# Where the last raw block of the values lies, and when a block of output weights is opened, in a fused attention and gated-attention layer

## The chip, the cores and the metric

The kernel runs on one core of a Trainium2 chip. The metric is the device time of one execution in microseconds (us); lower is better. Three executions of the kernel before took 981.74, 981.85 and 983.63 us; the median, 981.85 us, is the number to compare with. A further execution was taken with the hardware profiler.

## The reference

One decoder layer over 1024 tokens of width 1024, in fp32. The input is normalized and multiplied by one wide matrix `w_in`; the columns of the product are the queries, keys, values and gates of eight differential softmax heads (`qa, ka, va, ga`) and of four gated linear heads (`qb, kb, vb, gb`, and a low-rank decay). Both results go through the output matrix and are added to the input:

```python
h = rms_norm(x, pre_g)
z = jnp.einsum('bsd,de->bse', h, w_in)
qa, ka, va, ga, qb, kb, vb, gb, gk_low = split_columns(z)
...
oa = diff_attention(qa, ka, va, lam)                 # softmax(q1 k1) - lam * softmax(q2 k2), times v
oa = rms_norm(oa, subln_g) * (1.0 - lam_init) * silu(ga)
log_a = log_sigmoid(gk_low @ w_gk_up + b_gk) / 16
ob = gla_chunked(qb, kb, vb, log_a)                  # S_t = diag(exp(log_a_t)) S_{t-1} + k_t^T v_t; o_t = q_t S_t
ob = rms_norm(ob, gla_g) * silu(gb)
y = jnp.einsum('bse,ed->bsd', jnp.concatenate([oa, ob], axis=-1), w_out)
return x + rms_norm(y, post_g)
```

## The kernel before

**Stages.** First the projections `h @ w_in` (until about 634 us of the span), with the gated heads computed in between; then scores, softmax and values of the eight attention heads together with the output product; then the last norm.

**Precision.** Every fp32 operand is split into a rounded part and a rest (`hi`, `lo`), and a product is three TensorE passes: hi with hi, hi with lo, lo with hi. A split takes a cast on ScalarE (ACT) and a subtraction on VectorE (DVE).

**Steps.** A projection is cut into 26 groups of columns (`pairs`, p = 0 to 25). Each is done by seven products instead of eight (a Strassen scheme) over the four quarters b11, b12, b21, b22 of its weights; `order` lists the steps (p, n), n = 1 to 7. A product n has its own left block of `h` and its own sum of weight quarters: n = 1 uses b11, n = 2 uses b21, n = 5 uses b12 - b11, n = 6 uses b22 - (b12 - b11), n = 7 uses b22 - b12, n = 4 uses b21 less the sum of n = 6, n = 3 uses b22. `go` (L682) runs the list: it makes the weights of up to three steps ahead (`prepare`), issues the matmuls of the step (`step`), lets `wo_step` do a piece of the output weights, and lets the generator `gla` of the gated heads do a piece.

**Values.** p = 22 and 23 (`VALS`) are the values of the attention heads. Both share one set of weights: eight raw loads of 512 KB, a half [0] and a half [1] of each of b11, b21, b12, b22 (`load_values`, L202, the DMA is L214, on SyncE's queue SP). `value_weights` (L291) makes the sums in place (L302, DVE), casts each half to hi (L306, ACT) and subtracts for lo (L309, DVE). hi and lo lie in a ring of five slots (`NRING`); a step's two hi and two lo take four of them, and a slot is free when the matmuls of both p = 22 and 23 that read it are done. `multiply_values` (L384) uses hi in its first two passes of eight matmuls and lo in the third.

**Places in memory.** The pool `kp` has the tags q0, q1, k0, k1, ks0, ks1 with one buffer each. They hold different tiles in turn; a new tile of a tag waits until every access to the one before it is done. During the gated heads q1 holds the decayed queries `gqd` (its other half serves `wo_step` as scratch, `spare`), ks0 the output `o` of the gated head ("go" in the profile), k1 a chain of small tiles that ends with the squares `sq_hl`, ks1 the gates ("gg"), q0 and k0 the keys, queries and values (`kq`, `gv`). The values' b12 goes to q0 and k0 and b22 to k1 and ks0. `o` is free when its last stores to `mixe` (L944) have landed; `gqd` is free when the last output matmul of the last gated head ("gpo") and the last use as scratch are done. At n = 7 the values keep two snapshots in `s3` (L483): in ks1 for p = 22, in q1 for p = 23. The same six tags then take the first attention head's queries and keys (`load_qk`, L954).

**Output weights.** `wo_step` (L663) splits `w_out` ahead of time in 32 blocks of 256 KB: one load into the single buffer `wo_raw` (L679, on GpSimd's queue POOL), a cast (L667, ACT), a subtraction (L669, DVE) and two stores to a DRAM copy (L671, POOL). A block is opened (loaded) at one step and closed (the rest) at a later one. Before the gated heads have begun, blocks are opened at n = 2 or 4 and closed at n = 1 or 6, and lo is written back into `wo_raw`, so that the next load waits for the store. Once `gqd` exists, lo goes to its free half, and each step with n = 1 or 6 closes one block and opens the next. The gated heads start right after the step (9, 3), that is at (10, 2).

**Order on the engines.** Matmuls are pinned in program order, and each block's load is pinned behind what precedes it on POOL. All other instructions are put in order by a planner that plays the program through on a timeline of its own, so an instruction stands in its engine's queue where the planner believed it would be ready. Each engine then runs its queue strictly in that order.

Of the kernel before, what the change touches and what calls it, by code (L numbers as in the profile page):

```python
# [8 lines left out]
F32 = mybir.dt.float32  # L9
# [5 lines left out]
P = 128  # L15
# [16 lines left out]
def hymba_kernel(  # L32
# [77 lines left out]
    def take_bank(shape, name):  # L110
        i = free.pop(0)
        return bank(i, shape, name), i
# [40 lines left out]
    kp = ctx.enter_context(tc.tile_pool(name="kp", bufs=1))  # L153
# [3 lines left out]
    def t2k(tag, bufs, name, dt=F32, shape=(P, 512)):  # L157
        return ap.tile(list(shape), dt, tag=tag, name=name, bufs=bufs)
# [17 lines left out]
    VALS = (len(pairs), len(pairs) + 1)  # L176
# [8 lines left out]
    def load_raw(p, halves=(0, 1)):  # L185
        if p >= len(pairs):
            return
        if p in VALS:
            return load_values("b11")
        c0 = pairs[p][2]  # L190
        for kh in halves:
            if kh not in raws.setdefault(p, {}):
                r = ap.tile([P, HB, 256], F32, tag="raw", name="w_raw", bufs=4)
                rows = slice(kh * 512, kh * 512 + 512)
                sp.dma_start(r, w_in[0, rows, c0 : c0 + 256].rearrange("(k p) c -> p k c", p=P))
                raws[p][kh] = r
# [5 lines left out]
    def load_values(name):  # L202

        if name not in value_raws:
            c0 = VA + (name[2] == "2") * 512
            r0 = (name[1] == "2") * 512
            value_raws[name] = []
            for i, tag in enumerate({"b12": ("q0", "k0"), "b22": ("k1", "ks0")}.get(name, ("raw",) * 2)):
                if tag == "raw":
                    r = ap.tile([P, 2, 512], F32, tag=tag, name="v_raw", bufs=4)  # L210
                else:
                    r = kp.tile([P, 2, 512], F32, tag=tag, name="v_raw")
                rows = slice(r0 + i * 256, r0 + i * 256 + 256)
                sp.dma_start(r, w_in[0, rows, c0 : c0 + 512].rearrange("(k p) c -> p k c", p=P))  # L214
                value_raws[name].append(r)

    EARLY = 5
    order = [(0, 1), (1, 1), (0, 2), (1, 2), (2, 1), (3, 1), (2, 2), (3, 2), (4, 1), (4, 2)]
# [16 lines left out]
    i = order.index((1, 4))  # L235
# [22 lines left out]
    def prepare(i):  # L258

        if i >= len(order) or i in ws:  # L260
            return
        if i < 4:

            act_ins, dve_ins = normed[0][:2]
            with tc.issue_after(act_ins.ins), tc.issue_after(dve_ins.ins):
                make_weights(i)
        else:
            make_weights(i)
# [115 lines left out]
    def multiply_values(i, pss, start):  # L384

        p, n = order[i]
        hi, lo = H[LEFT[n]]
        w = ws.pop(i)
        for j, (a, b) in enumerate(((0, hi), (0, lo), (1, hi))):
            for k in range(HB):  # L390
                for u, ps in enumerate(pss):
                    c = ((p - VALS[0]) * 2 + u) * P
                    mm(
                        ps, at(b, k)[:, c : c + P], w[a][k // 2][:, k % 2, :],
                        start=(start and j == 0 and k == 0), stop=(j == 2 and k == HB - 1),
                        skip_group_check=True,
                    )
# [60 lines left out]
    def take_heads(tile, unit, p0, p1):  # L458

        c, hi = t_c("c"), t_st("v_hi", F32R)  # L460
        lo = c.bitcast(F32R)
        dve.tensor_tensor(c, p0, p1, ALU.add)
        act.copy(hi, c)
        dve.tensor_tensor(lo, c, fp(hi), ALU.subtract)
        for t, src in enumerate((hi, lo)):
            sp.dma_start(
                v_d[unit][:, t, :, tile, :].rearrange("u p c -> p u c"),
                fp(src).rearrange("p (u c) -> p u c", c=P),
            )
# [3 lines left out]
    def step_values(i):  # L473

        p, n = order[i]
        state = sums.setdefault(p, [{}, {}])
        name = {1: "x", 2: "y", 5: "z", 6: "x", 4: "y", 7: "x", 3: "z"}[n]
        if n in (1, 2, 5, 4):
            for b in state:
                b[name], b["i" + name] = take_bank([P, 512], name)  # L480
        multiply_values(i, [b[name] for b in state], n not in (6, 7, 3))
        if n == 7:
            s3 = kp.tile([P, 2, 512], F32, tag="ks1" if p == VALS[0] else "q1", name="s3")  # L483
        for u, b in enumerate(state):
            t = (p - VALS[0]) * 2 + u
            ps = b[name]
            if n in (1, 6):
                k = "s1" if n == 1 else "s2"
                b[k] = t2k("s", 4, "s")
                act.copy(b[k], ps)  # L490
            elif n == 7:
                b["s3"] = s3[:, u]
                act.copy(b["s3"], ps)
                free.append(b["ix"])
                take_heads(4 + t, 1, b["z"], b["s3"])
            elif n != 5:
                half, unit, k = {2: (0, 0, "s1"), 4: (1, 0, "s3"), 3: (0, 1, "s2")}[n]
                take_heads(half * 4 + t, unit, ps, b[k])
                free.append(b["i" + name])

    def step(i):

        p, n = order[i]
        if p in VALS:
            return step_values(i)
        kind, m, _ = pairs[p]
        def snap(k, ps):
            other = k == "s3" and (wide(p) or p >= len(pairs) - 2)
            b[k] = t_c("s") if other else t2k("s", 4, "s")
            act.copy(b[k], ps)  # L510

        b = sums.setdefault(p, {})
        name = {1: "x", 2: "y", 5: "z", 6: "x", 4: "y", 7: "x", 3: "z"}[n]
        if n in (1, 2, 4, 5):
            b[name], b["i" + name] = take_bank([P, 512], name)
        ps = b[name]
        multiply(i, ps, n not in (6, 7, 3))

        def done(half, unit, p0, p1):
            if wide(p):  # L520
                return take_values(p, half, unit, p0, p1)
            c = t_c("c")
            dve.tensor_tensor(c, p0, p1, ALU.add)
            take(kind, m, half, unit, c)

        if n == 1:
            snap("s1", ps)
        elif n == 2:
            done(0, 0, ps, b["s1"])
            free.append(b["iy"])  # L530
        elif n == 6:
            snap("s2", ps)
        elif n == 7:
            snap("s3", ps)
            free.append(b["ix"])
            done(1, 1, b["z"], b["s3"])
            done(1, 0, b["y"], b["s3"])
            free.append(b["iy"])
        elif n == 3:
            done(0, 1, ps, b["s2"])  # L540
            free.append(b["iz"])
# [121 lines left out]
    def wo_step(n):  # L663
        if n in (1, 6) and wo_open:
            e, dh, raw = wo_open.pop()
            hi = t_c("wo_hi", F32R)
            act.copy(hi, raw)  # L667
            lo = (spare[0][:, 1] if spare else raw).bitcast(F32R)
            dve.tensor_tensor(lo, raw, fp(hi), ALU.subtract)  # L669
            for t, src in enumerate((hi, lo)):  # L670
                pool.dma_start(wod[e][t][:, cols(dh)], fp(src))  # L671
        if n in ((1, 6) if spare else (2, 4)) and wo_todo and not wo_open:
            e, dh = wo_todo.pop(0)
            raw = ap.tile([P, 512], F32, tag="t4", name="wo_raw", bufs=1)
            src = w_out[0, e * P : (e + 1) * P, cols(dh)]
            if len(wo_todo) == 31:
                sp.dma_start(raw, src)
            else:
                tc.keep_in_program_order(pool.dma_start(raw, src))  # L679
            wo_open.append((e, dh, raw))  # L680

    def go(n):  # L682
        for _ in range(n):
            i = made[0]
            if i == len(order):
                return
            made[0] = i + 1
            for a in range(4):
                prepare(i + a)
            step(i)  # L690
            if order[i][0] >= EARLY and order[i][0] not in VALS:
                wo_step(order[i][1])
            for _ in range(2 if order[i][0] in VALS else 1):
                if fill and next(fill[0], 0) == 0:
                    fill.pop(0)
# [3 lines left out]
    for i in range(1, 4):  # L699
        prepare(i)  # L700
    go(1)
    first(1)
    go(2)
    norm_x(4, 5)
    norm_x(6, 7)
    go(1)
    for j in range(HB):
        blocks(j)
# [905 lines left out]
```

## Time and profile before

| | |
|---|---|
| median of three executions | 981.85 us |
| the profiled execution | 983.51 us, of which its span (first to last instruction) 981.8 us |
| TensorE (PE) busy | 954.9 us, 97% |
| VectorE (DVE), ScalarE (ACT), GpSimd (POOL) busy | 734.3, 602.6, 187.7 us |
| mean granted TensorE clock | 0.997 |
| DMA | 220.39 MB, mean 224 GB/s |

How to read the rows further down. A row of a timeline has the start and the length in us, the engine, the line, the operation, its output and inputs, and how many were merged ("x8"); in brackets stands how long the engine had been idle before it and what ended that. "SPq" and "POOLq" are the queues that issue DMAs; the length there is the issue, not the transfer. A row of waits has who waited for whom, the us in total, how often, and the longest. A row of windows has the window, its length, the busy time of each engine, then the granted TensorE clock (1.00 is full speed), the share of the DMA engines and GB/s. A row of the chain of waits has start, length and what the last-ending work was at that time.

### The profile page before, as it was taken

The numbers are of one execution on the slowest core, as the hardware profiler recorded it, in microseconds if no ns is written. First come the engines' busy times: TensorE is split into PE (matmuls) and PEld (weight loads), VectorE is DVE, ScalarE is ACT, GpSimd is POOL, SyncE is SP. The second block draws the span as 40 slices with busy tenths as digits, with TensorE's granted clock in tenths as the row PEclk, the third lists the DMA queues.
The fourth block names the chain that finished last, engine by engine and source line by source line (L and its number), as shares of the span: only waits on it lengthen the run. The fifth ranks groups of instructions, "written<-read, shape, count | busy, mean of one in ns | idle before, by whom it ended". The sixth has DMA issues, their size and how long they took to land.

```text
span 981.8 us, 14991 instructions
## 1 busy us (share of the span) xinstructions
PE 954.9 (97%) x4946; PEld 812.4 (83%) x4946; DVE 734.3 (75%) x1452; ACT 602.6 (61%) x1164; POOL 187.7 (19%) x253
## 2 busy tenths in 40 slices
PE   6999999998999999999999899999999999999997
PEld 5998988887888888888888688878888888888785
DVE  6887598896677787677666567487888888898554
ACT  8642454754667456567665244366777687787773
POOL 5200001111111111122100002121322322343321
PEclk9999999999999999999999999999999999999999
DMA  9442456477676979886663489997746659995777
GB/s 353 141 117 89 133 171 221 172 234 279 216 234 217 306 240 305 274 281 224 235 193 108 140 249 282 396 281 239 234 153 231 230 200 359 341 282 115 150 204 150
DMA packets 152141, 220.39 MB, mean 224 GB/s; under 512 B 16592, under 2 KB 87248, under 8 KB 151968
## 3 DMA queue, kind: packets, MB, share of 16 engines
q1 hardware_dynamic: 138128, 178.80, 56.7%
q0 software_dynamic: 13936, 40.64, 13.9%
q8 instruction: 39, 0.64, 0.3%
q14 instruction: 38, 0.31, 0.1%
HBM read 133.93 MB, written 88.60 MB: 227 GB/s over the span
## 4 chain that ended last, share of the span: by engine, by line
PE 83%; DMA 6%; issue 4%; DVE 4%; ACT 1%; POOL 1%; SPq 0%; DVEq 0%; POOLq 0%; ACTq 0%
PE x L117 20%; PE ypart L117 13%; PE y L117 12%; PE z L117 11%; PE sc L117 7%; PE po L117 5%; PE yps L117 4%; PE wtr L120 3%; PE gpo L117 3%; DMA wo_d<-wo_raw 3%; DMA wo_raw<-in_w_out_dram 2%; PE kv L117 1%; DMA w_raw<-in_w_in_dram 1%; PE gkl_ps L117 1%; PE pa L117 1%
## 5 line engine op out<-in xcount | busy, mean ns | idle before, releaser
L352 ACT CAST w<-w_raw 128x512 fp32r<-128x512 f32 (+1 forms) x150 | 98.0, 655 | 99.1 <-PE y L117 42.3
L353 DVE TENSOR_TENSOR w<-w_raw,w 128x512 fp32r<-128x512 f32 (+1 forms) x150 | 109.6, 732 | 40.2 <-ACT w L352 39.6
L1137 ACT ACTIVATE p<-p,stt 128x896 f32<-128x896 f32 (+7 forms) x128 | 99.3, 777 | 36.8 <-DVE stt L1127 35.7
L510 ACT COPY s<-x 128x512 f32<-128x512 f32 x72 | 42.2, 586 | 71.3 <-PE x L117 71.0
L1127 DVE CUSTOM_DVE_ANT_0 p<-sc,maskt 128x512 f32<-128x512 f32 (+3 forms) x128 | 74.2, 585 | 14.3 <-PE sc L117 12.8
L1143 POOL TENSOR_SCALAR p<-p,stt,lam 128x1024 f32<-128x1024 f32 (+3 forms) x64 | 56.5, 882 | 146.5 <-DVE stt L1142 144.7
L117 PE MATMUL x<-s_hi,w 128*128 128x512 f32 x320 | 80.2, 393 | 2.5 <-ACT s L510 2.5
L117 PE MATMUL z<-s_hi,w 128*128 128x512 f32 x320 | 80.1, 392 | 0.0
L117 PE MATMUL y<-h_hi,w 128*128 128x512 f32 x320 | 80.0, 392 | 0.0
L117 PE MATMUL ypart<-wo_hi,m_hi 128*128 128x512 f32 x192 | 79.5, 414 | 0.1
L671 POOL DMA_DIRECT2D wo_d<-wo_hi x32 | 17.6, 551 | 318.6 <-ACT wo_hi L667 318.6
L117 PE MATMUL ypart<-wo_hi,m_lo 128*128 128x512 f32 x192 | 75.5, 393 | 0.0
L117 PE MATMUL ypart<-wo_lo,m_hi 128*128 128x512 f32 x192 | 75.4, 393 | 0.0
L333 DVE TENSOR_TENSOR w_raw<-w_raw 128x512 f32<-128x512 f32 (+1 forms) x88 | 65.6, 746 | 10.6 <-DMA w_raw<-in_w_in_dram 9.4
L117 PEld LDWEIGHTS x<-s_hi,w 128*128 128x128 f32 x320 | 59.6, 188 | 15.1 <-ACT s L510 2.9
L117 PE MATMUL sc<-k,q 128*128 128x512 f32 (+1 forms) x192 | 69.0, 363 | 1.3 <-DVE stt L1127 1.3
L117 PEld LDWEIGHTS y<-h_hi,w 128*128 128x128 f32 x320 | 59.7, 188 | 12.2
L117 PEld LDWEIGHTS z<-s_hi,w 128*128 128x128 f32 x320 | 59.6, 188 | 12.2
L117 PE MATMUL sc<-ks,q 128*128 128x512 f32 (+1 forms) x192 | 66.1, 347 | 0.0
L1185 ACT CAST wt_hi<-wtr 128x512 fp32r<-128x512 f32 (+1 forms) x80 | 42.8, 535 | 25.5 <-PE wtr L120 24.8
L1186 DVE TENSOR_TENSOR wt_lo<-wtr,wt_hi 128x512 fp32r<-128x512 f32 (+1 forms) x80 | 50.6, 632 | 9.0 <-ACT wt_hi L1185 8.5
L1146 DVE SCALAR_TENSOR_TENSOR p<-p,stt,p 128x1024 f32<-128x1024 f32 (+3 forms) x64 | 52.1, 814 | 5.1 <-POOL p L1143 4.8
(236 smaller groups left out, 2307.7 us busy)
## 6 DMA issues: line engine op xcount, KB each, us to landing
w_raw<-in_w_in_dram SPq DMA_DIRECT2D x48, 512.0 KB, 4.7
wo_d<-wo_hi POOLq DMA_DIRECT2D x32, 256.0 KB, 2.9
q<-q_d SPq DMA_DIRECT2D x32, 256.0 KB, 4.8
k<-k_d SPq DMA_DIRECT2D x32, 256.0 KB, 5.7
ks<-k_d SPq DMA_DIRECT2D x64, 128.0 KB, 5.7
v<-v_d SPq DMA_DIRECT2D x16, 512.0 KB, 6.8
wo_raw<-in_w_out_dram POOLq DMA_DIRECT2D x31, 256.0 KB, 4.3
wo_d<-gqd POOLq DMA_DIRECT2D x22, 256.0 KB, 3.8
```

The costliest lines, as they stand in the source:

```text
L117: tc.keep_in_program_order(pe.matmul(*a, **k))
L120: tc.keep_in_program_order(pe.transpose(dst, src, ident))
L333: dve.tensor_tensor(dst, a, b, ALU.subtract)
L352: act.copy(w[0], src)
L353: dve.tensor_tensor(w[1], src, fp(w[0]), ALU.subtract)
L510: act.copy(b[k], ps)
L1127: ins = dve.tensor_tensor_reduce(p[:, a:e], sc[:, : e - a], maskt[:, NZ + P - (e - a) :] if last else maskt[:, : e - a], 1.0, 3e38 if i == ...
L1137: act.activation(p[:, :n], p[:, :n], AF.Exp, bias=st[:, m : m + 1], scale=-1.0, accum_out=st[:, 2 + m : 3 + m],)
L1143: pool.tensor_scalar(p1[:, :n], p1[:, :n], st[:, 5:6], lam, ALU.mult, ALU.mult)
L1146: dve.scalar_tensor_tensor(p0[:, :n], p0[:, :n], st[:, 4:5], p1[:, :n], ALU.mult, ALU.subtract)
L1185: act.copy(hi[:, :n], pt[:, :n])
L1186: dve.tensor_tensor(lo[:, :n], pt[:, :n], fp(hi[:, :n]), ALU.subtract)
```

## The change

Three lines. The second half of the values' b22 goes to the buffer q1 instead of ks0. The snapshot `s3` of p = 23, which was in q1, goes to ks0. And `wo_step` is left out at the step (9, 4), where it opened a block four steps ahead of the gated heads.

```diff
-            for i, tag in enumerate({"b12": ("q0", "k0"), "b22": ("k1", "ks0")}.get(name, ("raw",) * 2)):
+            for i, tag in enumerate({"b12": ("q0", "k0"), "b22": ("k1", "q1")}.get(name, ("raw",) * 2)):
...
-            s3 = kp.tile([P, 2, 512], F32, tag="ks1" if p == VALS[0] else "q1", name="s3")
+            s3 = kp.tile([P, 2, 512], F32, tag="ks1" if p == VALS[0] else "ks0", name="s3")
...
-            if order[i][0] >= EARLY and order[i][0] not in VALS:
+            if order[i][0] >= EARLY and order[i][0] not in VALS and order[i] != (9, 4):
                 wo_step(order[i][1])
```

In terms of blocks: with the blocks counted from 0, block 9 was opened at (9, 4) and closed at (10, 1), and block 10 was opened at (10, 2). Now block 9 is opened at (10, 2), and every later block moves up by one place in the list of steps. Block 31, which was opened at (20, 6) and closed at (21, 1), is opened at (21, 1) and closed at (21, 6). The number of blocks, loads and stores stays the same.

## The prediction

> **What bounds the kernel now.** I read the page's first line and its chain first, then what PE waits for, then the neighbourhood of each long wait.
>
> ```profile
> PE 954.9 (97%) x4946; PEld 812.4 (83%) x4946; DVE 734.3 (75%) x1452; ACT 602.6 (61%) x1164; POOL 187.7 (19%) x253
> PE 83%; DMA 6%; issue 4%; DVE 4%; ACT 1%; POOL 1%; SPq 0%; DVEq 0%; POOLq 0%; ACTq 0%
> ```
>
> PE is the bound: an edit pays only where PE stands still. The waits of PE, longest first:
>
> ```profile
> PE xT L120 <- DVE x L565: 8.7, 4, 7.3
> PE x L117 <- ACT w L306: 3.8, 1, 3.8
> PE x L117 <- ACT s L510: 2.5, 1, 2.5
> ```
>
> The first is the start of the kernel. The two others lie where this change works: ACT w L306 casts a weight of the values, ACT s L510 copies a sum next to the output weights. PE around the first of them:
>
> ```profile
> 543.60 1.98 PE L117 MATMUL z<-w,s_lo 128*128 128x512 f32 x8
> ...
> 547.23 1.07 PE L117 MATMUL x<-w,s_hi 128*128 128x512 f32 x4
> 552.10 1.65 PE L117 MATMUL x<-w,s_hi 128*128 128x512 f32 x4 [3.80 <-ACT w L306]
> ...
> 556.55 3.81 PE L117 MATMUL x<-w,s_hi 128*128 128x512 f32 x16
> ```
>
> From 543.60 to 547.23 run sixteen matmuls (eight of them in the row left out): 3.63 / 16 = 0.227 us each. The values' product n = 6 begins at 547.23, runs four matmuls on the first half of its weights, to 547.23 + 0.91 = 548.14, and stands until the second half is cast. The next starts at 552.10: **3.96 us idle**. Then twelve matmuls take 556.55 - 552.10 = 4.45 us where 2.72 would do: **1.73 us more**. The windows say why:
>
> ```profile
> 548.00:552.00 4.00, 0.30 (x2) 0.00 (x0) 2.31 (x3) 1.00 (x2) 0.00 (x0) 1.00 0.16 61
> 552.00:556.00 4.00, 3.90 (x10) 3.11 (x11) 3.46 (x4) 1.00 (x2) 0.00 (x0) 0.58 0.11 20
> ```
>
> The granted clock after the gap is 0.58; 4.00 x 0.42 = 1.68 us of pulses are missing, which fits. Together the place costs 3.96 + 1.73 = 5.69 us. What it waits for, in the chain of waits:
>
> ```profile
> 543.08 2.25 DMA mixe<-go
> ...
> 545.40 4.27 DMA v_raw<-in_w_in_dram
> ...
> 551.00 1.05 ACT w L306
> ```
>
> The last store of the gated heads' output must land before ks0 may be overwritten; only then, at 545.40, goes the load of b22[1]; DVE makes the sum, ACT casts it, PE goes on.
>
> **The change, part by part.**
>
> *b22[1] into q1.* The last reader of q1, and the loads of b12[1] and b22[0]:
>
> ```profile
> 516.40 0.39 PE L117 MATMUL gpo<-gqd,gu 128*128 128x128 f32 x2
> ...
> 516.60 0.38 SPq L214 DMA_DIRECT2D v_raw<-in_w_in_dram  x1
> ...
> 531.01 0.38 SPq L214 DMA_DIRECT2D v_raw<-in_w_in_dram  x1
> ```
>
> q1 is read for the last time at 516.40 + 0.39 = 516.8; k0 comes free with the same matmuls, and b12[1] leaves for it at 516.60. The scratch half of q1 is done with earlier (below). So b22[1] can leave right behind b12[1], or, if the planner keeps the order of the code, right behind b22[0] at 531.4. Its flight is bounded by the eight loads of this kind:
>
> ```profile
> DMA to landing us min/median/max: 3.6/3.9/5.5
> ```
>
> It lands by 531.4 + 5.5 = 536.9. What is late next? DVE:
>
> ```profile
> 538.30 1.22 DVE L309 TENSOR_TENSOR w<-v_raw,w 128x1024 fp32r<-128x1024 f32 x1
> ...
> 541.23 1.22 DVE L302 TENSOR_TENSOR v_raw<-v_raw 128x1024 f32<-128x1024 f32 x1
> ...
> 544.17 1.22 DVE L302 TENSOR_TENSOR v_raw<-v_raw 128x1024 f32<-128x1024 f32 x1
> 549.69 3.50 DVE L302 TENSOR_TENSOR v_raw<-v_raw 128x1024 f32<-128x1024 f32 x3 [4.30 <-DMA v_raw<-in_w_in_dram]
> 553.10 2.35 DVE L309 TENSOR_TENSOR w<-v_raw,w 128x1024 fp32r<-128x1024 f32 x2
> ```
>
> By the order of the code I read 538.30 as the last use of the old sum in b11[1], 541.23 as the first half of the new one, and the first of the three at 549.69 as the half that PE lacks. The bracket at 549.69 says that DVE stood 4.30 us for the load, so it was at work until 545.39. If the planner now puts the missing sum right behind 541.23, it ends at about 543.7; if it puts it at the end of that run, at 545.39 + 1.22 = 546.6. The cast (1.05) needs a ring slot as well: the first to come free is that of n = 5's first half, four matmuls into the pass at 543.60, at 544.5. So the second half is ready between 544.5 + 1.05 = 545.6 and 546.6 + 1.05 = 547.7, and PE wants it at 548.14. The lo halves follow: behind 546.6 one more sum (1.22), then two subtractions, the first done at 549.0, the second at 550.2. PE's third pass starts at 547.23 + 16 x 0.227 = 550.9 and wants the second half 0.9 later. **PE does not stop, and the 5.69 us go whole**; the tightest margin is 0.4 us. If DVE does one more sum first (the third of 549.69 may come early now), PE stands 1.22 - 0.4 = 0.8 us.
>
> Would a shorter rest of the gap also pay for the clock? The other gap, before 226.38, did not:
>
> ```profile
> 226.00:230.00 4.00, 3.62 (x16) 3.02 (x17) 3.24 (x5) 1.94 (x5) 1.09 (x3) 1.00 0.53 210
> ```
>
> So 2.50 us of waiting left the clock at 1.00 and 3.96 us of idling did not; by the rows a rest of 3 us would cost between 3.0 and 4.7. The Trainium skill, "TensorE: Matmul & The Clock Gate", section "What's actually happening", lets the clock fall after about 3.4 us of idling; by that a rest of 3 us would cost 3.0, the lower end. Both gaps here agree with it.
>
> *s3 into ks0.* The snapshot of p = 23 is written here:
>
> ```profile
> 574.67 0.59 ACT L493 COPY s<-x 128x512 f32<-128x512 f32 x1 [1.39 <-PE x L117]
> ```
>
> ks0's stores have landed by 545.4, so it waits for nothing. Afterwards q1 and ks0 have changed roles under the first attention head's loads, which may move one of them by a microsecond or two. The cover is long, from the last issue (593.32 + 1.97 = 595.3) to the first use:
>
> ```profile
> 593.32 1.97 SPq L966 DMA_DIRECT2D ks<-k_d  x3
> ...
> 636.29 0.40 PE L117 MATMUL sc<-k,q 128*128 128x512 f32 x1
> ```
>
> *No block at (9, 4).* The blocks run late on their one buffer:
>
> ```profile
> L671 POOL DMA_DIRECT2D wo_d<-wo_raw x10: 539/539/567, 143.5 to 234.9; - x10
> ...
> 229.98 0.55 POOL L679 DMA_DIRECT2D wo_raw<-in_w_out_dram  x1 [2.59 <-DMA wo_d<-wo_raw]
> ...
> 239.95 0.55 POOL L679 DMA_DIRECT2D wo_raw<-in_w_out_dram  x1 [4.53 <-DMA wo_d<-wo_raw]
> ```
>
> Ten stores leave `wo_raw`, those of blocks 0 to 9, the last at 234.9; so 229.98 is block 9's load and 239.95 block 10's. Block 9 with its load, cast, subtraction and two stores now belongs to (10, 2) and (10, 6), and block 10 no longer waits 4.53 us for a store. ACT's casts of blocks 8 and 10:
>
> ```profile
> 225.22 0.62 ACT L667 CAST wo_hi<-wo_raw 128x512 fp32r<-128x512 f32 x1 [6.12 <-DMA wo_raw<-in_w_out_dram]
> ...
> 244.50 0.62 ACT L667 CAST wo_hi<-wo_raw 128x512 fp32r<-128x512 f32 x1 [2.22 <-DMA wo_raw<-in_w_out_dram]
> ```
>
> PE's 2.50 us before 226.38 come from the first: it stands in ACT's queue ahead of the copy that PE needs. But that is block 8, opened at (9, 2), ahead of the edit, and the planner works forward in time; I take the stall as unchanged, **0**, with -2.5 us if those two change places and +2.5 if such an order arises anew. The wait at 244.50 should shrink; PE did not wait there, and gains nothing.
>
> At the far end block 31 comes four steps later, about where these stand:
>
> ```profile
> 489.01 0.54 POOL L671 DMA_DIRECT2D wo_d<-gqd  x1 [0.95 <-DVE gqd L669]
> ...
> 506.49 0.62 ACT L352 CAST w<-w_raw 128x512 fp32r<-128x512 f32 x1 [4.85 <-PE x L117]
> wo_raw<-in_w_out_dram POOLq DMA_DIRECT2D x31, 256.0 KB, 4.3
> ```
>
> Its load can leave behind 489.01 and is there by about 494. ACT has 4.85 us free before 506.49 for one cast. Stores that leave by 507.5, with the load's 4.3 us for their flight, are down by 512, before the 516.8 at which q1 comes free anyway. Without that cover b22[1] would still have until 531.
>
> *Sum.* -5.69 + 0 + 0. The profiled execution took 983.51 us with a span of 981.8: 983.51 - 5.69 = 977.8, span 976.1. The median of the runs is 1.66 us lower: 981.85 - 5.69 = **976.2 us**. Behind 552 no wait of PE is longer than those quoted at the top, and the later loads hang on PE's own progress, so the gain is kept.
>
> **Rivals.**
>
> *Part is lost to crowding.* b22[1] beside b12[1] delays the latter, and DVE's and ACT's queues stand behind it:
>
> ```profile
> 520.17 1.23 DVE L302 TENSOR_TENSOR v_raw<-v_raw 128x1024 f32<-128x1024 f32 x1 [7.19 <-DMA v_raw<-in_w_in_dram]
> ...
> 523.69 1.03 ACT L306 CAST w<-v_raw 128x1024 fp32r<-128x1024 f32 x1
> ...
> 524.80 1.98 PE L117 MATMUL y<-w,h_hi 128*128 128x512 f32 x8
> ```
>
> Behind 520.17 comes the sum of the gated head's squares, behind its cast on ACT the cast at 523.69, done at 524.7; PE wants that half four matmuls after 524.80, at 525.7. If both loads shared evenly, b12[1] would land 3.6 us later and PE stand 3.6 - 1.0 = 2.6 us: 978.8, or 980.5 if the clock falls too. Against: SP issues b12[1] first. With the 0.8 us of DVE above, this case is 977 to 980.5; chance 0.15. The Trainium skill, "DMA: Bandwidth & Descriptors", section "Bandwidth", measures 6.15 us for 1 MB; by that, as an estimate, the slip would be 2.5 us and PE's loss 1.5. No pair of such loads stands alone in this trace.
>
> *The stall at 226 goes too*, by a new order on ACT: 976.2 - 2.5 = 973.7; chance 0.07.
>
> *The change doesn't do what it says.* The load may use q1 but keep its place in SP's queue, behind these stores:
>
> ```profile
> 543.68 1.13 SPq L466 DMA_DIRECT2D v_d<-c  x2
> ```
>
> It would leave at 544.8, 0.6 us earlier than now: 981.2. For: the queue's order is the planner's. Against: b12[1] left within 0.2 us of its buffer's release. Chance 0.08.
>
> *Slower.* The planner deals the casts L667 of blocks 9 to 31 anew, and they stand in front of a copy L510 while their block has not landed, as block 8's does. Place: ACT's queue from 226 to 506; price 2.5 us each; it outweighs the gain from the third on (3 x 2.5 = 7.5). Four would give 976.2 + 10 = 986.2. Against: from (10, 6) on the steps that open and close are the same as before, and of the two late loads quoted only one stopped PE. Chance 0.10.
>
> **How the numbers follow.** Forecast, chance 0.60: 976.2, by itself 975.2 to 977.2 (DVE's 0.8 us and as much the other way). The range, 973.4 to 980.6, reaches from the stall at 226 to crowding with the clock, and leaves out the case of no effect and the slower one (0.18). A measurement of this kernel can tell about 0.2% (2 us) from no change. Faster by more than that: the forecast, the stall at 226 and most of crowding, 0.81. Within it: no effect and the rest of crowding, 0.09. Slower: 0.10.
>
> **What would show it.** Right: a load L214 leaves between 516 and 532 and none behind the `mixe` stores; no wait of PE on ACT w L306; the clock is 1.00 from 540 to 560; nine stores out of `wo_raw`. Wrong: a wait of PE between 517 and 530 (crowding), on L510 at a new place (dealing), or near 548 for DVE's sums.

## The result and the profile after

Six executions of the changed kernel took 974.86 to 978.85 us, **median 977.18 us**; six of the kernel before took 981.74 to 983.63 us, median 982.57. The ratio is **0.9944, 95% interval 0.9928 to 0.996**: 5.4 us less, with 3.9 to 7.1 us inside the interval. The forecast was 976.2 us within 973.4 to 980.6, and faster. The profiled execution of the changed kernel took 977.31 us, with a span of 975.6 us and a mean granted clock of 0.997; before these were 983.51, 981.8 and 0.997.

The page's first line and its chain, after (PEld is TensorE's loading of weights):

```profile
PE 953.7 (98%) x4946; PEld 811.4 (83%) x4946; DVE 734.2 (75%) x1452; ACT 602.7 (62%) x1164; POOL 188.1 (19%) x253
...
PE 84%; DMA 5%; issue 4%; DVE 4%; ACT 1%; POOL 1%; SPq 0%; DVEq 0%; POOLq 0%; ACTq 0%
```

The same number of instructions on every engine, nearly the same busy times: no work was removed, PE only stands less. Its waits, after:

```profile
PE xT L120 <- DVE x L565: 8.8, 4, 7.1
PE x L117 <- ACT s L510: 1.9, 1, 1.9
PE y L117 <- DVE s L648: 1.3, 1, 1.3
```

The wait on the values' cast (w L306), the second longest before, is no longer there. The one on the copy (s L510) is. The timeline of PE at the values' n = 6, after:

```profile
545.46 1.98 PE L117 MATMUL z<-w,s_hi 128*128 128x512 f32 x8
547.28 1.98 PE L117 MATMUL x<-w,s_hi 128*128 128x512 f32 x8
549.09 1.98 PE L117 MATMUL x<-w,s_lo 128*128 128x512 f32 x8
```

n = 6 begins at 547.28 (547.23 before) and now runs eight matmuls through where it ran four and stood. The windows of after, one ahead of it and two on the stretch that was lost before (the busy times are those of PE, PEld, DVE, ACT and POOL, in this order):

```profile
544.00:548.00 4.00, 4.00 (x20) 3.30 (x19) 4.00 (x6) 1.58 (x2) 0.00 (x0) 1.00 0.69 205
548.00:552.00 4.00, 4.00 (x19) 3.34 (x18) 2.00 (x2) 0.53 (x1) 0.00 (x0) 1.00 0.51 147
552.00:556.00 4.00, 4.00 (x19) 3.30 (x19) 0.00 (x0) 1.44 (x3) 0.00 (x0) 1.00 0.38 119
```

PE is busy for 4.00 of 4.00 us at clock 1.00; before, the second window held 0.30 us of work and the third ran at 0.58. The cause is in SP's queue, after:

```profile
516.67 0.90 SPq L214 DMA_DIRECT2D v_raw<-in_w_in_dram  x2
...
531.09 0.37 SPq L214 DMA_DIRECT2D v_raw<-in_w_in_dram  x1
...
543.14 0.36 SPq L944 DMA_DIRECT2D mixe<-go  x1
```

At 516.67 leave two raw loads where before there was one: b12[1] and right behind it b22[1]. Behind the last `mixe` store no load L214 follows.

**Where the 6.2 us of the spans come from.** Setting the start of every matmul beside that of the same matmul before gives the running difference: -0.94 us from the first 20 us on (the start of the kernel, which differs from execution to execution), **+1.01 us at the stall near 226**, **-5.72 us at the values' n = 6**, -0.5 us when the attention heads begin, near 657. The sum is -6.2. The second term shows a flaw in my reading; here is its place after, first PE, then its windows:

```profile
221.87 1.07 PE L117 MATMUL y<-h_lo,w 128*128 128x512 f32 x4
224.82 2.62 PE L117 MATMUL x<-s_hi,w 128*128 128x512 f32 x8 [1.89 <-ACT s L510]
```

```profile
222.00:226.00 4.00, 2.12 (x10) 1.42 (x9) 1.37 (x3) 2.15 (x4) 1.08 (x2) 1.00 0.99 353
226.00:230.00 4.00, 4.00 (x13) 3.13 (x12) 2.19 (x5) 0.81 (x2) 0.55 (x1) 0.57 0.40 149
```

PE waited less than before (1.89 us, not 2.50), but this time the granted clock behind it fell to 0.57: 4.00 x 0.43 = 1.7 us of pulses are missing.

### The profile page after: what moved, and what is told of

The parts are those of the page before. It is cut to its first block, busy times and chain, and to the rows that moved or that the text cites. A ratio compares the mean times of both kernels' runs of the same rounds, so it can differ in the third digit from the quotient of the medians.

```text
span 975.6 us, 14993 instructions
## 1 busy us (share of the span) xinstructions
PE 953.7 (98%) x4946; PEld 811.4 (83%) x4946; DVE 734.2 (75%) x1452; ACT 602.7 (62%) x1164; POOL 188.1 (19%) x253
## 4 chain that ended last, share of the span: by engine, by line
PE 84%; DMA 5%; issue 4%; DVE 4%; ACT 1%; POOL 1%; SPq 0%; DVEq 0%; POOLq 0%; ACTq 0%
PE x L117 20%; PE ypart L117 13%; PE y L117 12%; PE z L117 12%; PE sc L117 7%; PE po L117 5%; PE yps L117 4%; PE wtr L120 3%; PE gpo L117 3%; DMA wo_d<-wo_raw 2%; PE kv L117 1%; DMA wo_raw<-in_w_out_dram 1%; PE gkl_ps L117 1%; PE pa L117 1%; DMA k_d<-qk_st 1%
## 5 line engine op out<-in xcount | busy, mean ns | idle before, releaser
L510 ACT COPY s<-x 128x512 f32<-128x512 f32 x72 | 42.2, 586 | 73.9 <-PE x L117 73.4
L117 PE MATMUL x<-s_hi,w 128*128 128x512 f32 x320 | 80.7, 394 | 1.9 <-ACT s L510 1.9
L117 PE MATMUL z<-s_hi,w 128*128 128x512 f32 x320 | 80.1, 392 | 0.0
L117 PE MATMUL y<-h_hi,w 128*128 128x512 f32 x320 | 80.0, 392 | 0.0
L117 PE MATMUL ypart<-wo_hi,m_hi 128*128 128x512 f32 x192 | 79.6, 414 | 0.1
L117 PE MATMUL ypart<-wo_hi,m_lo 128*128 128x512 f32 x192 | 75.5, 393 | 0.0
L117 PE MATMUL ypart<-wo_lo,m_hi 128*128 128x512 f32 x192 | 75.4, 393 | 0.0
L117 PEld LDWEIGHTS x<-s_hi,w 128*128 128x128 f32 x320 | 59.8, 188 | 14.6 <-ACT s L510 2.3
L117 PE MATMUL sc<-k,q 128*128 128x512 f32 (+1 forms) x192 | 69.0, 363 | 1.2 <-DVE stt L1127 1.2
L117 PEld LDWEIGHTS y<-h_hi,w 128*128 128x128 f32 x320 | 59.7, 188 | 12.2
L117 PEld LDWEIGHTS z<-s_hi,w 128*128 128x128 f32 x320 | 59.6, 188 | 12.2
L117 PE MATMUL sc<-ks,q 128*128 128x512 f32 (+1 forms) x192 | 66.1, 347 | 0.1
```

What stands on the lines that cost most here:

```text
L117: tc.keep_in_program_order(pe.matmul(*a, **k))
```

## The experiments

The theory T: the gain is the values' stop alone, made by the first two lines of the change (the buffers); the third line is worth nothing by itself, and the stall near 226 is a separate matter that the change leaves alone. The rivals: the third line has a part in the gain, by fewer waits for the stores (R1); or what matters is only that the load comes earlier at all, so that a load that still leaves behind the stores would do nearly as well in another buffer (R2). Each ratio is to the kernel before on the same chip in the same series. No kernel leaves work out.

### The parts alone

`e1_b22_only` keeps the two lines on the buffers and takes the third back; `e2_wo_only` is the reverse.

```diff
 e1_b22_only, against the changed kernel
-            if order[i][0] >= EARLY and order[i][0] not in VALS and order[i] != (9, 4):
+            if order[i][0] >= EARLY and order[i][0] not in VALS:
 e2_wo_only, against the changed kernel
-            ... {"b12": ("q0", "k0"), "b22": ("k1", "q1")} ...
+            ... {"b12": ("q0", "k0"), "b22": ("k1", "ks0")} ...
-            s3 = kp.tile([P, 2, 512], F32, tag="ks1" if p == VALS[0] else "ks0", name="s3")
+            s3 = kp.tile([P, 2, 512], F32, tag="ks1" if p == VALS[0] else "q1", name="s3")
```

> Only the two buffer lines of the change; the block of output weights is still opened at (9, 4). If the whole gain is the load of b22[1] that no longer waits for the gated heads' stores, this kernel gains as much as the full change, 5.7 us against the kernel before (5 to 6.5): PE has no wait on ACT w L306 near 548, the clock is 1.00 from 540 to 560, and the load leaves right behind b12[1] near 517. If the block of output weights carries part of the gain, this one falls short by that part (over 1 us).

> Only the third line: no block at (9, 4); b22[1] stays in ks0. If that line is worth nothing, the time is that of the kernel before (within 1 us), PE's wait of 3.8 us at 552 is still there with the clock near 0.6 behind it, and the wait near 226 stands as well. If the line carries part of the gain, 1 to 3 us faster. ACT's wait of 2.2 us for a block at 244.5 should be gone either way.

Measured: **e1 976.84 us, ratio 0.9917 (0.9898 to 0.9937); e2 984.53 us, ratio 1.0 (0.9986 to 1.0014)**. By the medians e1 gained 7.3 us, more than the 5 to 6.5 expected. The longest waits of PE in e1, then those in e2 behind the start of the kernel:

```profile
PE xT L120 <- DVE x L565: 8.9, 4, 7.5
PE x L117 <- ACT s L510: 2.2, 1, 2.2
PE y L117 <- DVE s L648: 1.3, 1, 1.3
```

```profile
PE x L117 <- ACT w L306: 3.7, 1, 3.7
PE x L117 <- ACT s L510: 2.9, 2, 2.4
```

With the buffers alone the wait on w L306 is gone; with the third line alone it is all there. The median of e1 may have come out well or badly by the spread of single executions, so both were run again in another series: the change itself twice (`e5_change_again`, `e9_change_third`), the buffers alone once (`e10_buffers_again`, the kernel of e1).

> The full change once more, beside the next three on one chip. If the third line of the change (no block at (9, 4)) is worth nothing, this kernel and the two buffer lines alone differ only in how deep the stall near 226 falls in a run. 5 to 7.5 us faster than the kernel before: 5.7 for the load, and up to 1.7 either way for the clock behind 226.

> The full change, beside the two buffer lines alone on the same chip: 5 to 7.5 us faster than the kernel before, and within 1.5 us of the next kernel if the third line is worth nothing by itself.

> The two buffer lines alone, again. Earlier they came out at 0.9917 of the kernel before, the full change at 0.9944 and 0.9942, on other chips. If that was the spread of the stall near 226, both are within 1.5 us here; if the third line costs something, this kernel is again 2 us faster than the full change.

Measured: e5 977.81 us, ratio 0.9942 (0.992 to 0.9964); e9 977.43, 0.9943 (0.9924 to 0.9962); e10 977.03, **0.994 (0.9918 to 0.9962)**. Three series of the change agree to 0.0002, and side by side on one chip the buffers alone give the same as all three lines. T stands, and R1 falls for the change as made: without the third line no loss is seen and with it alone no gain, as far as intervals of some 2 us either way can tell.

### Is it the wait for the stores?

`e3_late_load` keeps the new buffers and holds b22[1]'s load back on SP's queue until the last `mixe` store has been issued. The load then waits for no buffer, only for its place in the queue. `e6_late_by_less` holds it back behind the last but two of those stores.

```diff
-        for name in {1: ("b11", "b21"), 2: ("b12",), 5: ("b22",), 3: ()}.get(n, ()):
+        for name in {1: ("b11", "b21"), 2: ("b12",), 5: ("b22",), 6: ("late",)}.get(n, ()):
...
+                with tc.issue_after(mixes[-1].ins) if name == "late" else nullcontext(): sp.dma_start(r, ...)
```

("late" is the half of b22 in q1; `mixes` collects the stores L944. e6 has `mixes[-3]`.)

> The full change, but the load of b22[1] (into q1, as in the change) is queued on SP right behind the last store of the gated heads' output instead of being issued near 517. If the gain is only the time at which this load leaves, it leaves at 543.5, lands at 547.4 to 547.8, the sum ends at 549.0, the cast at 550.1, and PE stands 2.0 us: 2.0 us of the 5.7 are lost if the clock holds, 3.7 if it falls, so 2.0 to 3.7 us faster than the kernel before. If the gain comes from the other order of the buffers (s3 and q1 in new places) and not from the time of the load, this kernel is as fast as the full change (5.5 us).

> The full change with the load of b22[1] queued on SP behind the last but two of the gated heads' stores, about 1.7 us ahead of the place in the previous late load. If PE's stop follows the landing of the load one for one, it leaves 5.0 us ahead of the values' product n = 6, lands 3.9 to 4.7 us later, and the sum and the cast are done 1.2 to 2.0 us into that product, where PE wants them at 0.9: a stop of 0.3 to 1.1 us, the clock stays at 1.00, and the kernel is within 1.2 us of the full change. If any late load costs the same (a threshold rather than a slope), it is 3 to 4 us slower than the full change.

Measured: **e3 980.38 us, ratio 0.9957 (0.9942 to 0.9973)**, 3.5 us above e1 of the same series; **e6 978.33 us, ratio 0.9943 (0.9927 to 0.996)**, 0.5 us above e5 of its series. The load in e3 and its landing at DVE, the cast, then PE:

```profile
545.66 0.45 SPq L214 DMA_DIRECT2D v_raw<-in_w_in_dram  x1
```

```profile
550.38 3.50 DVE L302 TENSOR_TENSOR v_raw<-v_raw 128x1024 f32<-128x1024 f32 x3 [2.87 <-DMA v_raw<-in_w_in_dram]
```

```profile
548.95 1.07 PE L117 MATMUL x<-w,s_hi 128*128 128x512 f32 x4
552.80 1.21 PE L117 MATMUL x<-w,s_hi 128*128 128x512 f32 x4 [2.78 <-ACT w L306]
553.85 3.38 PE L117 MATMUL x<-w,s_lo 128*128 128x512 f32 x8
557.02 2.25 PE L117 MATMUL x<-w,s_hi 128*128 128x512 f32 x8
```

The load leaves at 545.66 and its half is there at 550.38, 4.72 us later. Four matmuls from 548.95 end at 549.86; PE stands until 552.80, 2.94 us, and the next twelve take 557.02 - 552.80 = 4.22 us where 2.72 would do, 1.50 more: 4.44 us in this execution. The stop is longer than the 2.0 us expected: the load left 3.29 us ahead of n = 6 (548.95 - 545.66) where 3.7 were assumed, and took 4.72 us where 3.9 to 4.3 were. Now e6, the load, its landing at DVE, PE:

```profile
540.98 0.53 SPq L214 DMA_DIRECT2D v_raw<-in_w_in_dram  x1
```

```profile
545.67 3.50 DVE L302 TENSOR_TENSOR v_raw<-v_raw 128x1024 f32<-128x1024 f32 x3 [1.10 <-DMA v_raw<-in_w_in_dram]
```

```profile
546.34 1.07 PE L117 MATMUL x<-w,s_hi 128*128 128x512 f32 x4
548.09 1.21 PE L117 MATMUL x<-w,s_hi 128*128 128x512 f32 x4 [0.68 <-ACT w L306]
```

546.34 + 0.91 = 547.25 to 548.09 is a stop of 0.84 us. So the time when the load leaves sets the stop, and the chain load, sum, cast, PE is the one that the forecast followed: a load that leaves 30.61, 5.36 and 3.29 us ahead of n = 6 (547.28 - 516.67, 546.34 - 540.98, 548.95 - 545.66) gives stops of 0, 0.84 and 2.94 us. From e6 to e3 the lead shrinks by 2.07 us and the stop grows by 2.10. R2 falls: a new buffer with the old departure keeps most of the loss.

### The stall near 226

On ACT the cast L667 of block 8 stands ahead of the copy L510 that PE waits for, and the cast waits for its block's load. ACT in the changed kernel:

```profile
223.67 0.62 ACT L667 CAST wo_hi<-wo_raw 128x512 fp32r<-128x512 f32 x1 [5.51 <-DMA wo_raw<-in_w_out_dram]
224.19 0.58 ACT L510 COPY s<-x 128x512 f32<-128x512 f32 x1
```

`e4_copy_first` is the changed kernel with that one cast fixed in its place in the program. In ACT's queue just these two instructions change places.

```diff
+    pin_cast = lambda ins: tc.keep_in_program_order(ins) if len(wo_todo) == 23 else ins
...
-            act.copy(hi, raw)
+            pin_cast(act.copy(hi, raw))
```

> The full change, and on ACT two neighbouring instructions change places: the copy of the sum that PE waits for near 224 goes ahead of the cast of output-weight block 8, whose load has not landed. Nothing else moves in any queue. If PE's wait of 1.9 us there (profile after) and the lower clock behind it (0.57 in 226 to 230) are both due to that order, this kernel is 2 to 3.8 us faster than the full change, 7.5 to 9.5 us faster than the kernel before, and has clock 1.00 from 222 to 232. If PE needs a weight that is cast behind block 8 just as soon, the wait only gets another name and the time is that of the full change.

Measured: 975.12 us, ratio 0.9906 (0.9886 to 0.9926). As it beats both kernels, it was run again beside the change, as `e11_copy_first_again`:

> The full change with the copy ahead of block 8's cast, again: 2 to 4 us faster than the full change on the same chip, with no wait of PE on ACT s L510 over 1 us between 222 and 250, where both kernels without the third line had one of 1.6 us at 246 (the cast of block 10 ahead of the next such copy).

Measured: **974.17 us (973.43 to 975.86), ratio 0.9915 (0.9899 to 0.993)**, 3.3 us below the change in the same series (e9, 977.43). In the series of e4, where the change itself was not run, e4 stands 1.7 us below e1. ACT in e11, then PE, then the windows:

```profile
220.48 0.59 ACT L510 COPY s<-x 128x512 f32<-128x512 f32 x1 [2.10 <-PE x L117]
223.07 0.62 ACT L667 CAST wo_hi<-wo_raw 128x512 fp32r<-128x512 f32 x1 [2.00 <-DMA wo_raw<-in_w_out_dram]
```

```profile
222.10 1.07 PE L117 MATMUL y<-h_lo,w 128*128 128x512 f32 x4
223.00 1.98 PE L117 MATMUL x<-s_hi,w 128*128 128x512 f32 x8
```

```profile
222.00:226.00 4.00, 4.00 (x20) 3.30 (x19) 2.65 (x5) 1.74 (x4) 1.08 (x2) 1.00 0.88 274
226.00:230.00 4.00, 4.00 (x19) 3.33 (x18) 3.97 (x8) 2.17 (x4) 0.55 (x1) 1.00 0.49 193
```

The cast still waits for its load, now 2.00 us, but the copy that PE needs has gone ahead of it, at 220.48, and PE runs through at clock 1.00. The spread of the six executions is 2.4 us, where those of e9, the change, span 5.4 us (974.95 to 980.38). That the stall makes the spread is not shown: e4, with the swap, spans 4.8 us (973.96 to 978.74), and e1, with the stall, 2.8 us (975.84 to 978.63). An extreme stall was caught in the profile of e5, an execution of 983.02 us, the longest of its six:

```profile
229.97 3.78 PE L117 MATMUL x<-s_hi,w 128*128 128x512 f32 x8 [4.36 <-ACT s L510]
```

Would the same swap have been worth as much in the kernel before, or without the third line? `e7_before_copy_first` is the kernel before with the swap, `e8_buffers_and_copy` the buffers and the swap without the third line.

> The kernel before with the two ACT instructions near 225 in changed order (copy first, then the cast of block 8) and nothing else. If the two stalls are independent and each costs its gap and the clock behind it, this one gains 2.7 to 4.5 us against the kernel before, and the stop at 552 with its low clock stays as it is. If the gain at one place is given back at the other (PE reaches the values earlier and waits longer there, because the stores it waits for do not move), less than 1 us.

> The two buffer lines alone with the copy ahead of the cast of block 8; the block at (9, 4) is opened as in the kernel before. If the gains add and the third line is worth nothing: 8 to 10 us faster than the kernel before, as the full change with the copy first was (9.0). If the third line is needed once the copy goes first (the blocks run even later on their buffer), a new wait of PE between 226 and 250 and 1 to 3 us less.

Measured: **e7 982.53 us, ratio 0.9985 (0.9974 to 0.9996)**; **e8 976.96 us, ratio 0.9927 (0.9907 to 0.9947)**. In the kernel before, the swap gave 1.35 us where the stall it removes had cost 2.5 or more; neither the 2.7 to 4.5 us nor the less than 1 us of the expectation came. ACT in e7, then PE in e8:

```profile
244.85 0.62 ACT L667 CAST wo_hi<-wo_raw 128x512 fp32r<-128x512 f32 x1 [5.16 <-DMA wo_raw<-in_w_out_dram]
245.37 0.58 ACT L510 COPY s<-x 128x512 f32<-128x512 f32 x1
```

```profile
247.26 2.11 PE L117 MATMUL x<-s_hi,w 128*128 128x512 f32 x8 [1.61 <-ACT s L510]
```

In both, the stall has moved on by two blocks: block 10's load waits for a store out of `wo_raw` and its cast blocks the next copy. So a part of R1 comes back: the third line is worth something, but only once the stall near 226 is gone. Block 10's load in e11, on POOL, shows how:

```profile
236.37 0.54 POOL L671 DMA_DIRECT2D wo_d<-gqd  x1 [0.27 <-DVE gqd L669]
236.90 0.55 POOL L679 DMA_DIRECT2D wo_raw<-in_w_out_dram  x1
```

It leaves right behind the stores of block 9, with no wait, because lo now lies in the scratch half. The trace prices this at 1.6 us; by the ratios e8 stands 1.2 us (e11) to 2.1 us (e4) above, in intervals that overlap.

Last, `e12_all_copies_first` fixes the cast of each block from 0 to 8 in the same way.

```diff
+    pin_cast = lambda ins: ins if spare else tc.keep_in_program_order(ins)
```

> The full change with the casts of all blocks that are opened before the gated heads (0 to 8) kept behind what precedes them on ACT, not only block 8's. If the casts of early blocks stall PE in some executions only (one stood 1.55 us at 167 in a profile of the full change), this is as fast as the previous kernel in most runs and with less spread: 973 to 976 when the kernel before has 982 to 984. If the new order of the planner costs more than it saves, it is slower than the previous kernel by over 1 us, with a wait of PE at a new place before 222.

Measured: 978.37 us, ratio 0.995 (0.9935 to 0.9965), 4.2 us above e11. The planner, held at nine places, dealt the rest anew, and another copy of the stall arose, on DVE and later (232) than expected (before 222); DVE's rows, then PE's wait:

```profile
228.74 0.69 DVE L669 TENSOR_TENSOR wo_raw<-wo_raw,wo_hi 128x512 fp32r<-128x512 f32 x1 [3.38 <-ACT wo_hi L667]
...
231.40 0.68 DVE L523 TENSOR_TENSOR c<-z,s 128x512 f32<-128x512 f32 x1
```

```profile
232.14 2.11 PE L117 MATMUL z<-s_hi,w 128*128 128x512 f32 x8 [3.07 <-DVE c L523]
```

The block's subtraction stands ahead of the sum that PE needs, and waits for the late cast. More pins are not better: the one that gained is the one whose pair the trace had named.

## Why the prediction was right, step by step

**b22[1] into q1, 5.69 us: right.** The forecast of 976.2 us took the kernel before at 981.85, the median of three; six have 982.57, which is most of the 1.0 us between 976.2 and the measured 977.18. Measured were 5.72 us at this place, and 5.2 to 7.3 us by the medians of the five comparisons of the new buffers, with and without the third line, against the kernel before (982.60 - 977.43 in the series of e9, 984.12 - 976.84 in that of e1), around the forecast. e3 and e6 show that the departure of the load is the cause; e1, e2 and e10 that no other line shares in it. Of the two departures that the working left open, the earlier one came true (behind b12[1]).

**The tightest margin, 0.4 us: too dark.** The sums and casts that matter, after:

```profile
543.03 1.22 DVE L302 TENSOR_TENSOR v_raw<-v_raw 128x1024 f32<-128x1024 f32 x1
```

```profile
542.61 1.05 ACT L306 CAST w<-v_raw 128x1024 fp32r<-128x1024 f32 x1 [1.17 <-DVE v_raw L302]
544.76 1.06 ACT L306 CAST w<-v_raw 128x1024 fp32r<-128x1024 f32 x1 [1.10 <-PE z L117]
```

The planner put the missing sum at 543.03, close behind the first half's, so it ended at 544.25. The cast waited for the ring slot ("PE z L117" in the bracket) until 544.76 and was done at 545.82: the lower end of the forecast's 545.6 to 547.7, and 2.4 us ahead of PE's 548.19.

**Crowding of b12[1]: hardly there.** The sum behind b12[1], after:

```profile
520.61 1.23 DVE L302 TENSOR_TENSOR v_raw<-v_raw 128x1024 f32<-128x1024 f32 x1 [6.87 <-DMA v_raw<-in_w_in_dram]
```

It begins 0.44 us later than before (520.17), though two loads of 512 KB left together; 0.07 us of that is the later departure. The rival's 3.6 us for an even sharing did not come, and PE did not stop. The load issued first goes nearly undisturbed: it lands 3.73 to 4.17 us after its issue in the nine traces with such a pair, and 3.56 to 3.66 us in the five in which b12[1] leaves alone. Nor did the 2.5 us come that I had estimated from the Trainium skill's 6.15 us for 1 MB ("DMA: Bandwidth & Descriptors", section "Bandwidth").

**s3 into ks0, and the far end of the output weights, 0: right.** No wait on either appears among PE's. The number of stores out of `wo_raw` is nine, as foretold:

```profile
L671 POOL DMA_DIRECT2D wo_d<-wo_raw x9: 542/542/569, 142.3 to 225.3; - x9
```

**No block at (9, 4), 0: right alone, incomplete.** e2 and e10 measured no effect. That the line covers the next stall as soon as the one near 226 is gone (e8 against e4 and e11) was not in the working.

**The stall near 226 and the clock: here a step failed.** "2.50 us of waiting left the clock at 1.00 and 3.96 did not" was a reading of one execution. I built on it that the stall costs a steady 2.50 us. In the traces at hand it waits 1.89 to 4.36 us and the clock may or may not fall behind it, so the stall costs from 2 to some 7 us from execution to execution. The forecast held all the same, because the stall stands in both kernels. That it weighs the same in both is not shown, with one trace of each run; the medians, 5.4 us apart where 5.69 were forecast, fit it.

What the clock goes by can be read from the kept traces. In all fourteen, from its first rise (17.4 to 20.4 us into the span, different in every execution) the granted clock changes only at ticks 3.413 us apart. Between the first matmuls and the last norm it is low, at 0.50, for one such step eight times and for two (6.83 us) twice, and the stretches at 1.00 are whole numbers of steps as well: 208.21 us, 61 steps, from the rise to the fall near 226 in seven traces. The stall near 226, cut at these ticks, before and then after:

```profile
221.56:224.97 3.41, 2.32 (x11) 1.58 (x9) 0.52 (x1) 0.00 (x0) 0.00 (x0) 1.00 1.03 367
224.97:228.38 3.41, 2.00 (x9) 1.67 (x10) 2.16 (x4) 2.14 (x4) 1.08 (x2) 1.00 0.85 319
```

```profile
222.84:226.25 3.41, 1.52 (x7) 1.19 (x7) 1.62 (x3) 2.15 (x4) 1.08 (x2) 1.00 1.00 359
226.25:229.67 3.42, 3.42 (x10) 2.68 (x9) 1.75 (x3) 0.48 (x1) 0.55 (x1) 0.50 0.33 119
```

Before, a tick cuts the stop in two: PE stands 3.41 - 2.32 = 1.09 us in one step and 1.41 in the next. After, all 1.89 us lie in one step. All 17 stops of PE over 1.5 us between the start of the kernel and the last norm, in the order of the longest idle time of PE within one step:

| kernel, place | PE's wait, us | most PE idle in one step, us | clock behind |
|---|---|---|---|
| e5, near 167 | 1.55 | 0.77 | 1.00 |
| e7, near 246 | 1.62 | 1.15 | 1.00 |
| before, near 226 | 2.50 | 1.41 | 1.00 |
| e6, near 226 | 1.95 | 1.51 | 1.00 |
| e8, near 247 | 1.61 | 1.60 | 1.00 |
| e7, values | 3.56 | 1.80 | 1.00 |
| changed, near 226 | 1.89 | 1.89 | 0.50 |
| e12, near 232 | 3.07 | 1.93 | 1.00 |
| e2, near 226 | 2.42 | 2.04 | 0.50 |
| e3, values | 2.78 | 2.08 | 0.50 |
| e2, values | 3.66 | 2.09 | 0.50, two steps |
| e1, near 226 | 2.18 | 2.18 | 0.50 |
| e9, near 226 | 2.28 | 2.27 | 0.50 |
| e5, near 226 | 4.36 | 2.33 | 0.50, two steps |
| before, values | 3.80 | 2.86 | 0.50 |
| e10, near 226 | 3.32 | 3.31 | 0.50 |
| e3, near 226 | 3.63 | 3.41 | 0.50 |

By the length of the wait the rows cannot be put in order; by the idle time within one step they can, up to one pair. The clock held at up to 1.80 us and fell from 2.04 us on; between them 1.89 fell and 1.93 held, and the ends of matmuls, which the profile models, are not sure to such a difference. A fall costs half of each low step in which PE works, up to 1.7 us. So the 2.50 us of before cost no clock because a tick happened to cut them. No run moved the ticks on purpose: the limit is read from these traces, not tested.

"A rest of 3 us would cost between 3.0 and 4.7" still held (e3: 4.44 in the trace, 3.5 in the medians). Beside it I had set the Trainium skill, "TensorE: Matmul & The Clock Gate", section "What's actually happening", by which the clock falls after an idle window of about 3.4 us, and the window is free-running. The traces agree with the window's length and with its running free. They do not bear out that it must be idle as a whole: in seven of the ten falls PE stood for only 1.89 to 2.33 us of the step ahead.

## What to carry to other kernels

When the bound engine stops for a load, follow the load back to its buffer, not to its size: here 512 KB left 29 us late because the tile before it in that buffer had to be stored first, and swapping two tags was worth 5.7 us. An instruction that waits for a transfer must not stand ahead of one that the bound engine needs on the same in-order engine; one swap of that kind was worth 1.7 and 3.3 us more in two series, but look for the next such pair behind it before you expect the whole price. And a gap's price with its clock is not read off one profile: here the same stop did or did not bring the clock down, by where the ticks of that execution cut it, so take several.

## What the hardware showed unexpectedly

- The granted clock of TensorE changes only at ticks 3.413 us apart, which lie differently in every execution. It fell to 0.50 for one or two steps when TensorE had stood 2.04 us or more of one step, and held at up to 1.80 us; so a stop of 1.89 us cost 1.7 us more (after), and one of 3.56 us, cut by a tick into 1.80 and 1.75, cost nothing more (e7).
- Two raw loads of 512 KB from one queue, some 0.5 us apart, delayed the first by about 0.4 us only.
